# Carried rows of three state arrays moved channel-major straight between memory and their tiles

## The chip, the cores and the metric

The kernel runs on all 8 cores of one Trainium2 chip. Each core takes one prompt sequence of 2,048 tokens and 16 of the 128 sample sequences (64 tokens), and no core waits for another. The metric is the device time of the slowest of the 8 cores, in microseconds (us). Five runs here fell in a second, slower state, in which two or four cores of one die show a lower granted TensorE clock (0.812 to 0.975, against 0.986 or more on the other cores) and the time was 761.16 to 882.82 us; such runs are named and left out of every comparison.

The engines are PE (TensorE; PEld is its weight load, which overlaps the matmuls: busy 338.0 us beside PE's 700.8 us in a span of 744.3 us), DVE (VectorE), ACT (ScalarE), POOL (GpSimd) and SP (SyncE, which here mainly issues DMA). "L455" is line 455 of the kernel. Several such lines are helpers, so the same line stands for many places: in the kernel before, L455 is every matmul, L463 every transpose on PE, L480 the three-operand DVE operation, L484 an elementwise operation of two tensors, L491 a DVE operation with per-channel scalars.

## The reference, cut to what matters

One layer of a decoder with three kinds of carried state. Sample sequences bring the last 15 rows of a pooling mixer, the last 2 rows of a short convolution and the last 2 rows of the up-projected FFN, and each of these is handed back, renewed:

```python
def causal_dwconv(p, w):             # carried rows stand in front of the new ones
    T = p.shape[1] - (CONV_W - 1)    # CONV_W = 3
    out = p[:, 0:T] * w[0]
    for k in range(1, CONV_W):
        out = out + p[:, k:k + T] * w[k]
    return out

# in the layer
h = rmsnorm(x, g_pre_mix) * (1 + sc1) + sh1
proj = h @ w_in
pool_in = jnp.concatenate([pool_buf, v_pool], axis=1)           # 15 carried rows, 512 channels
conv_in = jnp.concatenate([conv_buf, gate_c * x_conv], axis=1)  # 2 carried rows, 512 channels
...                                                             # mixers, output projection
h2 = rmsnorm(x, g_pre_ffn) * (1 + sc2) + sh2
up = h2 @ ffn_w_up                                              # 2 x 2816 channels
ffn_in = jnp.concatenate([ffn_buf, up], axis=1)                 # 2 carried rows, 5632 channels
a, b = jnp.split(causal_dwconv(ffn_in, ffn_conv_w), 2, axis=-1)
f = (jax.nn.silu(a) * b) @ ffn_w_down
return x, pool_in[:, -15:], conv_in[:, -2:], ffn_in[:, -2:]
```

## The kernel before

In memory the states lie row by row: a row is one position, its channels side by side. On the chip channels lie on partitions. So the kernel before turns every state on PE, in float32, through a PSUM bank, with a copy by ACT; outgoing rows are also gathered by POOL and staged for the store. The FFN state and the outgoing rows of the pool and conv states look like this (cut):

```python
def ffn_states(m, g0, g1):                         # FFN state in, two calls
    K.dma("sp", ... BIG[m] <- stf_d ...)           # cut: four loads into a spare tile
    for c0 in range(g0, g1, 4):
        b = take()
        tr([PSF[:, b, ...] for c in range(c0, c1)], [BIG[m][:, ...] ...], IDF, ...)   # turns on PE
        ...
        act(USB[:, ..., 0:2], PSF[:, b, ...], AF.Copy, [r_bank[b]], [r_usb], ...)
        give(b)

def turn_out(rows, ins, reads, st):                # pool and conv rows out
    b = take()
    tr([PSF[0:rows, b, m * 128:(m + 1) * 128] for m in range(4)], ins, IDF, ...)
    act(STGO[st][0:rows, :], PSF[0:rows, b, :], AF.Copy, [r_bank[b]], [r_stgo[st]], 512)
    give(b)
```

The up projection: one half is 16 matmuls into a pair of PSUM banks. ACT copies it, scaled by the last tap of the convolution, and DVE adds the two other taps with one operation of 1,023 columns and one of 1,022. Only after the second may PE write the pair again. Per channel pair i there are two halves, called a and b below, and then a gate product on POOL:

```python
def up_half(gi, i, ab):
    b = take_pair()
    for c in range(2):
        op = mm(PSF[:, b + c, :], [(W[:, kc, w0:w0 + 128], AH[:, kc, c0:c0 + 512]) for kc in range(KC)], ...)
    ...
    act(Tt, ps, AF.Copy, ..., scale=f[2])
    act(hd, ps[:, 1022:1024], AF.Copy, ...)
    stt(Tt[:, 1:1024], ps[:, 0:1023], f[1], Tt[:, 1:1024], ALU.mult, ALU.add, ...)   # 1023 columns
    stt(Tt[:, 2:1024], ps[:, 0:1022], f[0], Tt[:, 2:1024], ALU.mult, ALU.add, ...)   # 1022 columns
    give(b, b + 1)                                                                   # the pair is free
    ...

ma = up_half(gi, i, 0)
act(BIG[ma], BIG[ma], AF.Silu, ...)
mb = up_half(gi, i, 1)
tt(GB[:, i, 0:1024], BIG[ma], BIG[mb], ALU.mult, ..., eng="pool")                    # the gate product
```

DVE still modulates later tokens of `ah`, the normed input of the up projection (`ah * g + s`, 512 columns of bfloat16 at a time).

What DVE does first is not written down by hand. Every operation is recorded with a modelled cost, and a list scheduler inside the kernel plays the program through and sets each engine's order from that.

```python
HOP = {"pe": 0.20, "act": 0.20, "dve": 0.15, "pool": 0.20, "sp": 0.10}

def order(self):
    ...
    for o in reversed(self.all):
        need[o] = o.idx if o.eng == "pe" else min([far] + [need[u] for u in users[o]])
        o.key = (need[o], o.idx)          # the PE operation that needs it first
    ...
    def done(o):
        o.end = t
        for u in users[o]:
            waiting[u] -= 1
            if not waiting[u]:
                push(t + (0.0 if o.eng == u.eng == "pe" else self.HOP[o.eng]), "ready", u)
    ...                                   # a free engine takes the ready operation with the lowest key
```

In this model an operation that depends on the one before it on DVE becomes ready 0.15 us late, and the engine, free by then, takes another that is ready.

## Time and profile before

| what | value |
|---|---|
| time, 4 runs | median 746.51 us (745.71 to 747.77) |
| spans of the 8 cores in the profiled run | 738.6 to 744.3 us |
| PE busy, slowest core | 700.8 of 744.3 us |
| float32 turns on PE | 51 |

The busy line and the chain of the page of the kernel before. The chain is followed back from the last instruction to whatever released each step; the shares are of the span:

```profile
span 744.3 us, 12312 instructions; the slowest of 8 cores (738.6 to 744.3 us)
PE 700.8 (94%) x4051; PEld 338.0 (45%) x4051; DVE 465.8 (63%) x624; ACT 334.7 (45%) x591; POOL 277.2 (37%) x297
...
PE 91%; DMA 3%; DVE 2%; issue 2%; ACT 1%; DVEq 0%; SPq 0%; ACTq 0%; POOLq 0%
```

PE is the bound. The table of stretches of the kernel before says where it is not: each row is a stretch, its length, then the busy time of PE, PEld, DVE, ACT and POOL with the count of instructions, the granted clock, the DMA share and GB/s:

```profile
80.00:120.00 40.00, 32.77 (x251) 17.32 (x250) 34.70 (x60) 26.61 (x52) 18.09 (x25) 1.00 0.98 169
120.00:260.00 140.00, 139.45 (x880) 69.56 (x878) 88.93 (x165) 75.06 (x151) 71.31 (x103) 0.99 0.80 201
260.00:690.00 430.00, 429.43 (x2326) 201.82 (x2325) 291.36 (x289) 184.82 (x289) 157.49 (x94) 1.00 0.43 94
690.00:744.00 54.00, 48.57 (x228) 22.55 (x226) 12.27 (x18) 10.25 (x24) 11.69 (x5) 0.97 0.34 110
```

From 120 to 690 us PE rests about 1.1 us. What a turn costs there is read from the timeline of PE in the kernel before (start, duration, engine, line, operation, count; matmuls overlap, here 0.27 us long and 0.11 us apart, so a slot is the distance between starts):

```profile
141.70 0.27 PE L463 MATMUL ps<-idf_51,v_119 128*15 128x128 f32 x1
141.81 0.27 PE L463 MATMUL ps<-idf_51,v_121 128*15 128x128 f32 x1
...
142.14 3.62 PE L455 MATMUL ps<-ah_81,ring_71 128*128 128x512 bf16 x16
```

A turn lasts 0.27 us but takes a slot of 0.11 us: starts at 141.70 and 141.81, and after four of them the next matmul at 142.14.

```profile
286.69 2.40 POOL L484 TENSOR_TENSOR g_137<-big_79,big_80 128x1024 bf16<-128x1024 f32 x1 [4.20 <-DVE big_80 L480]
```

The half in big_75 is finished (1,023 and 1,022 columns) before the half in big_76 begins. The modulation piece that starts before POOL's gate product takes 0.40 us (286.46); the one that starts within it takes 1.26 us (287.98) and ends 0.15 us after it (289.24 against 289.09).

### The profile page before, as it was taken

To read this page: it belongs to the slowest core of one execution; us is meant where nothing else is said; L and a number is where in the kernel's file an instruction comes from. 1 tells how busy PE (TensorE), PEld (TensorE's weight loads), DVE (VectorE), ACT (ScalarE), POOL (GpSimd) and SP (SyncE) were. 2 spreads that over 40 slices of the span, in tenths; PEclk is the share of its full clock that TensorE was granted. 3 is DMA by queue.
4 is the path that set the end of the run, shared out by engine and by line. 5 is a ranking of instruction groups with operands and counts; after the bars stand their busy time and mean duration, and the time that the engine had idled before them with its cause. 6 is when DMAs were issued, how large, how long until landed. Compare 5 with 4: busy or idle time off the path is not lost.

```text
span 744.3 us, 12312 instructions; the slowest of 8 cores (738.6 to 744.3 us)
## 1 busy us (share of the span) xinstructions
PE 700.8 (94%) x4051; PEld 338.0 (45%) x4051; DVE 465.8 (63%) x624; ACT 334.7 (45%) x591; POOL 277.2 (37%) x297
## 2 busy tenths in 40 slices
PE   1589888999999999999999999999999999999996
PEld 1244434544455544444444444445444444444443
DVE  2448686745468889987777511138777777767212
ACT  4526754533467784455454311134444444423211
POOL 2312333323488654434444232224434242342320
PEclk9979999999999999999999999999999999999999
DMA  8999999499687653355878943113344333032522
GB/s 206 187 215 222 184 172 158 91 181 210 185 284 254 215 155 73 58 94 92 165 136 156 216 144 114 56 57 58 57 81 91 58 58 57 1 114 86 168 86 70
DMA packets 28225, 97.94 MB, mean 132 GB/s; under 512 B 3283, under 2 KB 7723, under 8 KB 24562
## 3 DMA queue, kind: packets, MB, share of 16 engines
q0 software_dynamic: 10944, 47.85, 37.7%
q1 hardware_dynamic: 17218, 49.31, 20.3%
q8 instruction: 33, 0.54, 0.3%
q14 instruction: 30, 0.25, 0.1%
HBM read 126.15 MB, written 19.19 MB: 195 GB/s over the span
## 4 chain that ended last, share of the span: by engine, by line
PE 91%; DMA 3%; DVE 2%; issue 2%; ACT 1%; DVEq 0%; SPq 0%; ACTq 0%; POOLq 0%
PE ps L455 87%; PE ps L463 2%; PE ps L682 2%; DMA big_77<-x 2%; DMA wsc_2_85<-w_sc 2%; DVE ah_81 L489 0%; DVE by_82 L480 0%; ACT ah_81 L476 0%; DVE ah_81 L601 0%; DVE ta_107 L480 0%; DVE xn_99 L489 0%; SPq L495 0%; DVE big_79 L480 0%; ACT xn_100 L476 0%; DVE xn_101 L489 0%
## 5 line engine op out<-in xcount | busy, mean ns | idle before, releaser
L455 PE MATMUL ps<-wdn_136,g_137 128*128 128x512 bf16 (+1 forms) x748 | 162.8, 379 | 0.0
L455 PE MATMUL ps<-ah_81,ring_72 128*128 128x512 bf16 (+2 forms) x816 | 151.1, 341 | 2.2 <-DVE by_82 L480 2.2
L455 PE MATMUL ps<-ah_81,ring_71 128*128 128x512 bf16 (+2 forms) x784 | 149.1, 345 | 3.0 <-DVE ah_81 L484 1.1
L455 PE MATMUL ps<-ah_81,ring_70 128*128 128x512 bf16 (+2 forms) x752 | 139.6, 339 | 1.5 <-DVE big_79 L480 0.6
L455 PEld LDWEIGHTS ps<-wdn_136,g_137 128*128 128x128 bf16 (+1 forms) x748 | 73.3, 99 | 86.7 <-issue 0.8
L455 PEld LDWEIGHTS ps<-ah_81,ring_72 128*128 128x128 bf16 x816 | 69.1, 98 | 79.0 <-issue 5.1
L455 PEld LDWEIGHTS ps<-ah_81,ring_71 128*128 128x128 bf16 x784 | 67.5, 98 | 77.4 <-issue 4.3
L455 PEld LDWEIGHTS ps<-ah_81,ring_70 128*128 128x128 bf16 x752 | 63.5, 98 | 70.6 <-issue 2.6
L573 DVE RECIPROCAL stat_55<-stat_55 128x1 f32<-128x1 f32 (+1 forms) x67 | 10.4, 157 | 124.4 <-ACT stat_55 L476 124.1
L484 POOL TENSOR_TENSOR g_137<-big_75,big_76 128x1024 bf16<-128x1024 f32 x15 | 35.3, 2355 | 63.1 <-DVE big_76 L484 33.7
L484 POOL TENSOR_TENSOR g_137<-big_77,big_78 128x1024 bf16<-128x1024 f32 x15 | 35.3, 2354 | 58.5 <-DVE big_78 L484 33.1
L484 POOL TENSOR_TENSOR g_137<-big_79,big_80 128x1024 bf16<-128x1024 f32 x14 | 33.0, 2359 | 55.5 <-DVE big_80 L484 27.9
L476 ACT ACTIVATE big_80<-ps 128x1024 bf16<-128x1024 f32 (+2 forms) x16 | 15.5, 968 | 75.3 <-PE ps L455 65.0
L480 DVE SCALAR_TENSOR_TENSOR big_75<-ps,vecs_43,big_75 128x1023 f32<-128x1023 f32 (+1 forms) x30 | 38.4, 1280 | 12.6 <-ACT halo_57 L476 4.9
L480 DVE SCALAR_TENSOR_TENSOR big_77<-ps,vecs_43,big_77 128x1023 f32<-128x1023 f32 (+1 forms) x30 | 38.4, 1281 | 12.1 <-ACT halob_58 L476 6.7
L480 DVE SCALAR_TENSOR_TENSOR big_76<-ps,vecs_43,big_76 128x1023 f32<-128x1023 f32 (+1 forms) x30 | 38.4, 1279 | 9.6 <-ACT halob_58 L476 4.2
L480 DVE SCALAR_TENSOR_TENSOR big_79<-ps,vecs_43,big_79 128x1023 f32<-128x1023 f32 (+1 forms) x28 | 35.8, 1280 | 12.9 <-ACT halob_58 L476 7.6
L480 DVE SCALAR_TENSOR_TENSOR big_78<-ps,vecs_43,big_78 128x1023 f32<-128x1023 f32 (+1 forms) x30 | 38.4, 1279 | 7.7 <-ACT halob_58 L476 3.5
L480 DVE SCALAR_TENSOR_TENSOR big_80<-ps,vecs_43,big_80 128x1023 f32<-128x1023 f32 (+1 forms) x28 | 35.8, 1280 | 8.3 <-ACT halob_58 L476 3.9
L476 ACT ACTIVATE big_79<-ps 128x1024 bf16<-128x1024 f32 x14 | 14.3, 1022 | 52.5 <-PE ps L455 51.6
L484 POOL TENSOR_TENSOR big_76<-big_80,big_76 128x256 f32<-128x256 f32 (+1 forms) x16 | 21.0, 1310 | 33.9 <-DVE big_80 L480 32.8
L484 POOL TENSOR_TENSOR big_75<-big_79,big_75 128x256 f32<-128x256 f32 (+1 forms) x16 | 19.6, 1227 | 34.2 <-DVE big_79 L480 23.2
(353 smaller groups left out, 933.6 us busy)
## 6 DMA issues: line engine op xcount, KB each, us to landing
ring_70<-w_up POOLq DMA_DIRECT2D x8, 1024.0 KB, 8.1
ring_71<-w_up POOLq DMA_DIRECT2D x7, 1024.0 KB, 8.4
ring_72<-w_up POOLq DMA_DIRECT2D x7, 1024.0 KB, 8.1
wdn_136<-w_down POOLq DMA_DIRECT2D x11, 512.0 KB, 12.1
y<-big_75 SPq DMA_DIRECT2D x7, 512.0 KB, 2.7
y<-big_76 SPq DMA_DIRECT2D x7, 512.0 KB, 2.7
y<-big_77 SPq DMA_DIRECT2D x7, 512.0 KB, 2.8
big_76<-x SPq DMA_DIRECT2D x6, 512.0 KB, 6.6
```

What stands on the lines that cost most here:

```text
L455: inst = e.matmul(bank_ap, l, r, start=(first and i == 0), stop=(last and i == len(pairs) - 1))
L463: inst = e.transpose(o, i, ident)
L476: return K.op("act", lambda e: e.activation(out=out, in_=in_, func=func, **kw), reads=reads, writes=writes, cost=c_act(n, ptr))
L480: return K.op(eng, lambda e: e.scalar_tensor_tensor(out, in0, s, in1, op0, op1), reads=reads, writes=writes, cost=c_dve(n))
L484: return K.op(eng, lambda e: e.tensor_tensor(out, in0, in1, op), reads=reads, writes=writes, cost=c_dve(n) if eng == "dve" else c_pool(n))
L573: K.op("dve", lambda e: e.reciprocal(STAT[0:rows, k + 1, t:t + 1], STAT[0:rows, k + 1, t:t + 1]), reads=[r_stat[k + 1][t]], writes=[r_stat ...
L682: inst = e.matmul(PSF[:, start_b[g, c], :], WINP[:, kc, g * 128:(g + 1) * 128], AH[:, kc, c * 512:(c + 1) * 512], start=(kc == 0), stop=(k ...
```

## The change

Its intent: the host lays the three states out channel by channel, so that each tile, with carried and new rows together, moves in one load and one store. Turns, their PSUM banks, ACT and POOL copies, staging, 16 small stores and a memory-to-memory copy of pool rows go. The price is bytes, since whole tiles travel with unused columns: the FFN state moves 2.16 MB each way instead of 0.72. The steps of the input projection are written as a list as well; the program order of the steps is as before, but every engine's order is computed anew. The core of the diff (cut):

```diff
-    stf_d = din("st_ffn", [NS * 2, 2 * DFF])
+    stf_d = din("st_ffn", [128, NCH * NS * (2 + DS)])
     ...                                              (likewise the pool and conv states, and all outputs)
-    def state_turns():  ...                          (8 turns: pool state in)
-    def conv_state_turn():  ...                      (4 turns: conv state in)
-    def ffn_states(m, g0, g1):  ...                  (11 turns: FFN state in)
+    def conv_state_in():
+        load(QS.rearrange("p j s r -> p (j s r)"), stc_d, [r_qs], 196608, deps=[conv_op[0, 0]])
+    def pool_state_in():
+        load(VS.rearrange("p g s r -> p (g s r)"), stp_d, [r_vs], 622592, deps=[conv_op[0, 4]])
+    def ffn_state_in():
+        load(USB.rearrange("p i a s r -> p (i a s r)"), stf_d, [r_usb], 2162688, deps=[up_op[-1]])
     ...
     def conv_states():                               (8 turns; pool_states likewise, 8 turns)
-        turn_out(2, [QLAST[:, j, :] for j in range(4)], r_ql, 2)
-        store(ncp_d, STGO[2][0:2, :], [r_stgo[2]], s_stgo[2])
-        new = SS[1][:, 0:8 * NS].rearrange("p (g s r) -> p g s r", g=4, r=2)
-        K.op("pool", lambda e: e.tensor_copy(new, QS[:, :, :, 4:6]), reads=[r_qs], writes=[r_ss[1]], cost=0.4)
-        turn_out(2 * NS, [SS[1][:, g * 2 * NS:(g + 1) * 2 * NS] for g in range(4)], [r_ss[1]], 0)
-        store(ncs_d, STGO[0][0:2 * NS, :], [r_stgo[0]], s_stgo[0])
+        store(ncp_d, QLAST.rearrange("p j r -> p (j r)"), r_ql, nbytes=4096)
+        store(ncs_d, QS.rearrange("p j s r -> p (j s r)"), [r_qs], nbytes=196608)
     ...
-                if i == NTAIL + 1:
-                    ffn_states(7, 0, 8)              (inside the first half of the up projection)
-                if i == NTAIL + 4:
-                    ffn_states(7, 8, 11)
     ...
         if step == 2:                                (inside the first down projection)
+            ffn_state_in()
     ...
-    def state_outs(xs):  ...                         (12 turns: FFN rows out)
+    def state_outs():
+        store(nfp_d, HALOB.rearrange("p r c -> p (r c)"), [r_halob], nbytes=45056)
+        store(nfs_d, USB.rearrange("p i a s r -> p (i a s r)"), [r_usb], nbytes=2162688)
```

## The prediction

> **What bounds the kernel.** TensorE. The page gives PE 700.8 us of a 744.3 us span (94%); the chain of waits is 91% PE. By the table of stretches the 43.5 us in which PE does not work are: 21.7 before 26.5 us (first loads), 7.7 up to 80 us, 7.2 from 80 to 120 us (DVE busy 34.7 of 40 us), about 1.1 from 120 to 690 us, 5.7 at the end. So after 120 us TensorE time taken out should come off the end.
>
> **What goes.** All 51 float32 turns of state. The groups say about 272 ns for one, which would make 14 us. [...] back to back, turns start every 0.11 us (141.70, 141.81, 141.92, 142.03, then the next matmul at 142.14). So they cost 51 x 0.11 = 5.6 us: conv in 0.44 at 70 us, pool in 0.82 at 114 us, pool out 0.88 at 142 to 146 us, conv out 0.88 at 195 us, FFN in 1.2 at 343 and 364 us, FFN out 1.3 at 689 and 695 us. Off the path go about 6 us of ACT copies, 5.3 us of POOL copies, 16 small stores that hold SP's queue 7 us from 148 us, and a 352 KB memory-to-memory copy.
>
> **What comes.** Tiles travel whole with unused columns: FFN 2.16 MB each way instead of 0.72, pool 0.62 MB, conv 0.20 MB. Conv and pool in, together 0.26 MB more, fall where the DMA engines are full (share about 1.0 from 10 to 130 us). The hardware queue moved 49.3 MB for 20.3% of 16 engines' span, so I estimate 0.8 us of all engines for it. Neither is urgent: conv state was ready at 71 us and first used at 84.9 us; pool state was issued at 83.8 us, landed within 13 us, and was turned at 114 us. The FFN state lands during the down projection (DMA share about 0.4); FFN rows may leave from 660 us, 80 us before the last store. The rewritten list of projection steps reads as the same order as before: no gain.
>
> **On the path.** The 39 turns after 120 us give 4.3 us; the 0.5 us wait before the conv rows' turns may go too. Of the 1.26 us before 120 us I count half, as DVE holds that stretch and a 2.17 us wait on DVE follows the pool turns. Sum about 5 us, less 0.3 us for fuller DMA queues. The order of issues and of PSUM banks is computed anew from a model inside the kernel, so the first 120 us may shift 2 us either way.
>
> **Predicted: 742.0 us, 738.5 to 745.0 in 8 of 10. Faster by over 2%: 3%; within 2%: 95%; slower by over 2%: 2%.**
>
> **What would show it.** No float32 turns on PE; PE busy about 6 us lower (near 694); PE idle between 120 and 690 us still about 1 us; the span about 4 us shorter between 120 us and the end, whatever the first 120 us do. If those gained more, the order of loads was the reason.
>
> **What would make it wrong.** A store that must land before its tile's space is reused (pool rows before the output weights, conv rows before x tiles) holding the POOL queue, which also computes; larger loads delaying x tiles or modulation weights in the full stretch; the 2.16 MB FFN load holding residual tiles behind it; turns that hid in waits I do not see.

The 5.6 us are 51 times the 0.11 us between starts in the timeline.

## More of the kernel before

The next two views are the stretch to compare later. First PE in the kernel before, from the turns of a bfloat16 tile at 267 us to 336 us:

```profile
267.23 0.61 PE L463 MATMUL ps<-idb_52,xn_100 128*128 128x128 bf16 x8
...
280.64 7.08 PE L455 MATMUL ps<-ah_81,ring_71 128*128 128x512 bf16 x32
287.56 13.98 PE L455 MATMUL ps<-ah_81,ring_72 128*128 128x512 bf16 x64
301.37 13.98 PE L455 MATMUL ps<-ah_81,ring_70 128*128 128x512 bf16 x64
315.19 13.98 PE L455 MATMUL ps<-ah_81,ring_71 128*128 128x512 bf16 x64
329.00 7.29 PE L455 MATMUL ps<-ah_81,ring_72 128*128 128x512 bf16 x33
```

Each row of 64 matmuls is four halves, and nothing stands in brackets after it: no wait that this view shows. Then the timeline of DVE in the same kernel, and below it one row of POOL's:

```profile
286.46 0.40 DVE L491 TENSOR_SCALAR ah_81<-ah_81,g2t_49,s2t_50 128x512 bf16<-128x512 bf16 x1
286.79 1.27 DVE L480 SCALAR_TENSOR_TENSOR big_75<-ps,vecs_43,big_75 128x1023 f32<-128x1023 f32 x1
287.98 1.26 DVE L491 TENSOR_SCALAR ah_81<-ah_81,g2t_49,s2t_50 128x512 bf16<-128x512 bf16 x1
289.16 1.27 DVE L480 SCALAR_TENSOR_TENSOR big_75<-ps,vecs_43,big_75 128x1022 f32<-128x1022 f32 x1
290.35 1.27 DVE L480 SCALAR_TENSOR_TENSOR big_76<-ps,vecs_43,big_76 128x1023 f32<-128x1023 f32 x1
```

## The result, and the profile after

The kernel after took 744.42 us (median of 4 runs, 743.72 to 745.17) against 746.51 us (4 runs, 745.71 to 747.77), a ratio of 0.9971 with a 95% interval of 0.9951 to 0.999. A ratio here is always the mean time of one kernel's fast runs over that of the other's of the same rounds, so it is not quite the ratio of the medians. The gain is about 2 us, less than half of what was predicted, and the time lies inside the range given.

The page of the kernel after, same lines as before:

```profile
span 742.2 us, 12030 instructions; the slowest of 8 cores (740.4 to 742.2 us)
PE 691.0 (93%) x3925; PEld 332.7 (45%) x4000; DVE 469.2 (63%) x624; ACT 328.1 (44%) x576; POOL 271.4 (37%) x293
...
PE 84%; DVE 5%; issue 5%; DMA 3%; ACT 1%; POOL 1%; DVEq 0%; SPq 0%; ACTq 0%; POOLq 0%
```

The weight loads fell from 4051 to 4000: exactly the 51 turns. The matmuls do not fit to that (3925), so 75 matmul records are missing from this trace and its PE busy time, 691.0, must not be compared with 700.8. The chain of waits is the better witness: PE's share of it fell from 91% to 84%, DVE's rose from 2% to 5% (that of "issue", which names no cause, rose as much).

The table of stretches after (same columns; the PE column is short of records here too):

```profile
80.00:120.00 40.00, 33.04 (x232) 16.70 (x237) 33.39 (x59) 25.43 (x51) 15.28 (x24) 0.96 1.04 186
120.00:260.00 140.00, 137.23 (x856) 68.36 (x870) 94.19 (x173) 75.64 (x152) 71.66 (x103) 1.00 0.81 202
260.00:690.00 430.00, 425.14 (x2264) 199.76 (x2307) 291.69 (x283) 182.02 (x282) 152.41 (x92) 1.00 0.49 104
690.00:744.00 54.00, 45.78 (x209) 20.97 (x211) 11.37 (x17) 7.34 (x18) 11.19 (x5) 0.98 0.26 88
```

Since weight loads are complete, they make a ruler without this flaw. The table below cuts each core's span at the first and last weight loads of the output projection and of the two down projections. All its rows but the start and the tail agree across the 8 cores of a run within 0.15 us, so they can be compared to a tenth; the tail differs by up to 0.5 us between cores after the change. Values are medians of the 8 cores of the profiled run.

| stretch, us | turns in it (before) | before | after | difference | predicted |
|---|---|---|---|---|---|
| start, to the output projection | 20 | 188.3 (185.2 to 190.9) | 188.6 (187.7 to 189.1) | see below | about -1.5 |
| output projection | 8 | 65.51 | 64.50 | -1.01 | -0.9 |
| first half of the up projection | 11 | 156.43 | 158.06 | **+1.63** | -1.2 |
| first down projection | 0 | 75.76 | 75.76 | 0.00 | 0 |
| second half of the up projection | 0 | 162.05 | 162.05 | 0.00 | 0 |
| second down projection | 12 | 87.30 | 85.99 | -1.31 | -1.3 |
| tail | 0 | 6.33 | 6.41 | +0.08 | 0 |

Here is the miss, in one row. The first half of the up projection (from the last weight load of the output projection to the first of the down projection) lost 11 turns and became longer. This is PE in that stretch after the change; a bracket is the time PE rested before a row, and what released it:

```profile
264.44 0.61 PE L476 MATMUL ps<-idb_52,xn_100 128*128 128x128 bf16 x8
...
284.77 3.62 PE L468 MATMUL ps<-ah_81,ring_72 128*128 128x512 bf16 x16
289.47 10.52 PE L468 MATMUL ps<-ah_81,ring_72 128*128 128x512 bf16 x47 [1.09 <-DVE big_75 L493]
299.83 3.62 PE L468 MATMUL ps<-ah_81,ring_70 128*128 128x512 bf16 x16
304.17 10.52 PE L468 MATMUL ps<-ah_81,ring_70 128*128 128x512 bf16 x47 [0.72 <-DVE big_79 L493]
314.52 3.62 PE L468 MATMUL ps<-ah_81,ring_71 128*128 128x512 bf16 x15
318.68 10.52 PE L468 MATMUL ps<-ah_81,ring_71 128*128 128x512 bf16 x47 [0.54 <-DVE big_77 L493]
329.04 7.29 PE L468 MATMUL ps<-ah_81,ring_72 128*128 128x512 bf16 x33
```

Compare the two ends with the view before. At the bfloat16 turns of xn_100 this core is 2.79 us ahead (264.44 against 267.23). At the last row it is level (329.04 against 329.00). In between three groups of 64 matmuls have each broken into 16 and 48 (a record or two are missing in each) with a wait for DVE. The brackets understate the waits, because ends of matmuls are modelled: between weight loads the gaps are 1.65, 1.28 and 1.10 us, where the usual distance is 0.22.

And this is the timeline of DVE in the kernel after, with one row of POOL's below it:

```profile
282.99 2.76 DVE L504 TENSOR_SCALAR ah_81<-ah_81,g2t_49,s2t_50 128x512 bf16<-128x512 bf16 x2
285.67 1.27 DVE L493 SCALAR_TENSOR_TENSOR big_75<-ps,vecs_43,big_75 128x1023 f32<-128x1023 f32 x1
286.87 1.27 DVE L493 SCALAR_TENSOR_TENSOR big_76<-ps,vecs_43,big_76 128x1023 f32<-128x1023 f32 x1
288.06 1.26 DVE L493 SCALAR_TENSOR_TENSOR big_75<-ps,vecs_43,big_75 128x1022 f32<-128x1022 f32 x1
289.25 1.26 DVE L493 SCALAR_TENSOR_TENSOR big_76<-ps,vecs_43,big_76 128x1022 f32<-128x1022 f32 x1
```

```profile
283.21 2.39 POOL L497 TENSOR_TENSOR g_135<-big_79,big_80 128x1024 bf16<-128x1024 f32 x1 [4.19 <-DVE big_80 L493]
```

Two things differ from before. The pieces are *crossed*: the 1,023 columns of big_76 now stand between the two pieces of big_75, so the PSUM pair of big_75 comes free one piece (1.2 us) later. And two modulation pieces in a row took 2.76 us: the first its usual time, while the second, alone in the trace from 283.31 to 285.75, began just after POOL's gate product and ended just after it (283.21 to 285.60). Measured from the start of the ring_72 matmuls, the pair came free after 2.87 us before (290.43 - 287.56) and after 4.55 us now (289.32 - 284.77), which is 1.68 us later. The 16 matmuls of the other half, which PE does meanwhile, take 3.45 us (a quarter of the 13.81 us between rows of 64): before, the pair was free in time, and now PE stood still until 289.47.

The crossing occurs at three pairs of halves, counted from 0 in program order: 6 and 7, 10 and 11, 14 and 15. The kernel before has none there. The full order of DVE in the trace adds a hint that no run tested: before, one modulation piece stands between the two pieces of nearly every half in this part; after, at the three places, two modulation pieces stand together in front of the halves, and none is left to stand between.

**Theory.** The turns did give back their slots, but the newly computed order crosses half-convolutions on DVE at three places and puts modulation pieces against POOL's gate product, and PE waits for PSUM there.

**Rivals.** (R1) The stretch is bound by DVE (busy 60.6 of the 65 us from 264 to 329 us before), so turns hid in DVE's time and taking them out frees nothing. (R2) The larger transfers hold others up. (R3) The order is accidental and a nudge of PE's modelled time restores it.

### The profile page after: what moved, and what is told of

Read it like the earlier page. It is cut to its first block, busy times and chain, and to the rows that moved or that the text cites. A ratio compares the mean times of both kernels' runs of the same rounds, so it can differ in the third digit from the quotient of the medians.

```text
span 742.2 us, 12030 instructions; the slowest of 8 cores (740.4 to 742.2 us)
## 1 busy us (share of the span) xinstructions
PE 691.0 (93%) x3925; PEld 332.7 (45%) x4000; DVE 469.2 (63%) x624; ACT 328.1 (44%) x576; POOL 271.4 (37%) x293
## 4 chain that ended last, share of the span: by engine, by line
PE 84%; DVE 5%; issue 5%; DMA 3%; ACT 1%; POOL 1%; DVEq 0%; SPq 0%; ACTq 0%; POOLq 0%
PE ps L468 81%; PE ps L695 2%; DMA wsc_2_85<-w_sc 2%; PE ps L476 2%; DMA big_77<-x 1%; DVE big_75 L493 1%; DVE big_79 L493 1%; POOL big_77 L497 0%; DVE ta_107 L493 0%; DVE big_80 L493 0%; DVE ah_81 L502 0%; DVE ah_81 L504 0%; ACT ah_81 L489 0%; DVE by_82 L493 0%; DVE xn_99 L502 0%
## 5 line engine op out<-in xcount | busy, mean ns | idle before, releaser
L468 PE MATMUL ps<-wdn_134,g_135 128*128 128x512 bf16 (+1 forms) x733 | 161.4, 379 | 0.9 <-issue 0.2
L468 PE MATMUL ps<-ah_81,ring_71 128*128 128x512 bf16 (+2 forms) x766 | 148.5, 346 | 5.6 <-DVE ah_81 L502 2.2
L468 PE MATMUL ps<-ah_81,ring_72 128*128 128x512 bf16 (+2 forms) x798 | 148.4, 338 | 2.2 <-DVE big_75 L493 1.1
L468 PE MATMUL ps<-ah_81,ring_70 128*128 128x512 bf16 (+2 forms) x739 | 138.0, 339 | 3.2 <-DVE ah_81 L502 0.9
L489 ACT ACTIVATE big_79<-ps 128x1024 bf16<-128x1024 f32 x14 | 14.3, 1023 | 55.8 <-PE ps L468 54.8
L497 POOL TENSOR_TENSOR big_75<-big_79,big_75 128x256 f32<-128x256 f32 (+1 forms) x16 | 20.0, 1250 | 49.6 <-DVE big_79 L493 30.9
L468 PE MATMUL ps<-wo_138,by_82 128*128 128x512 bf16 (+1 forms) x134 | 31.9, 379 | 0.1
```

Source lines behind the costliest of these rows:

```text
L468: inst = e.matmul(bank_ap, l, r, start=(first and i == 0), stop=(last and i == len(pairs) - 1))
L489: return K.op("act", lambda e: e.activation(out=out, in_=in_, func=func, **kw), reads=reads, writes=writes, cost=c_act(n, ptr))
L497: return K.op(eng, lambda e: e.tensor_tensor(out, in0, in1, op), reads=reads, writes=writes, cost=c_dve(n) if eng == "dve" else c_pool(n))
```

## The experiments

All kernels gave correct results. Two sessions were run, each on one chip and each with runs of the kernel before. In the first session (e1 to e4) the kernel before had a median of 746.28 us (5 fast runs; 2 slow ones of 815.51 and 882.82 are left out); in the second (e5 to e7 and after_again) 746.42 us (11 runs, 745.94 to 748.2). The first measurement above is apart from both. "The stretch" is the first half of the up projection, measured as in the table: 156.43 us before, 158.06 us after.

### e1_uncrossed: the kernel after, with the three crossings undone

```diff
+        dve = self.ops["dve"]
+        for k in (6, 10, 14):
+            b, a = self.halves[k][1], self.halves[k + 1][0]   # 1022 of one half, 1023 of the next
+            if dve.index(b) > dve.index(a):
+                dve.remove(b)
+                dve.insert(dve.index(a), b)
```

> The changed kernel with one edit: after the order of issue is computed, the three crossed pairs of half-convolutions on DVE in the first half of the up projection (a-first, b-first, a-second, b-second) are put straight (a-first, a-second, b-first, b-second). Nothing else moves. The stretch from the last weight load of the output projection to the first of the down projection was 156.4 us before and 158.1 us after, on all 8 cores. Theory A (the crossings hold PSUM pairs and so TensorE): the waits of 1.65, 1.28 and 1.10 us start-to-start shrink to under 0.5 us and the stretch is 155 to 155.6 us (before less the 1.2 us of turns); the whole kernel about 2.5 us faster than after (ratio to before about 0.993 to 0.995). Theory B (DVE is full in this stretch and TensorE waits for it in any order): the stretch stays within 0.7 us of 158.1.

Measured: the stretch 156.22 us, 1.84 us shorter; the other stretches as in the kernel after within 0.1 us. This lies between the two forecasts, nearer to theory A but outside its 155 to 155.6 us. Time 743.85 us, the median of the 3 fast runs (742.92 to 744.28, one slow run of 761.16 left out), ratio to the kernel before 0.996 (0.9936 to 0.9984). PE in this run (tile names have no numbers in the traces of experiments, and the lines lie a little lower with each edit):

```profile
280.51 10.53 PE L475 MATMUL ps<-ah,ring 128*128 128x512 bf16 x48
291.25 13.97 PE L475 MATMUL ps<-ah,ring 128*128 128x512 bf16 x64 [0.20 <-DVE big L500]
305.63 30.64 PE L475 MATMUL ps<-ah,ring 128*128 128x512 bf16 x141 [0.41 <-DVE big L500]
```

What follows: moving three DVE instructions ahead of a neighbour gives back 1.84 of the 2.83 us that the stretch lacks (158.06 less the 155.23 that it has in e5_ffn_in below, with its turns gone and nothing else). Crossing is a cause, but not all of it: gaps of 0.76 and 0.98 us stay at the first two places, and one of 0.45 us comes later, at 332.8 us.

### e2_crossed: the kernel before, with the same three pairs crossed

```diff
+        for k in (6, 10, 14):
+            b, a = self.halves[k][1], self.halves[k + 1][0]
+            dve.remove(b)
+            dve.insert(dve.index(a) + 1, b)
```

> The kernel before with one edit: after the order is computed, the same three pairs of half-convolutions on DVE (7th and 8th, 11th and 12th, 15th and 16th half) are crossed as they are after the change. All turns stay. Theory A: the stretch from output to down projection grows from 156.4 us by 1 to 3 us, with waits of TensorE on DVE at those three places, and nothing else changes. Theory B: it stays at 156.4 within 0.3 us.

Measured: the stretch 158.94 us, 2.51 us longer; all turns stay in. Time 751.2 us, the median of the 3 fast runs (748.18 to 751.55, one slow run of 778.97 left out), ratio 1.0052 (1.0018 to 1.0086). PE in this run:

```profile
282.94 10.53 PE L462 MATMUL ps<-ah,ring 128*128 128x512 bf16 x48
294.20 13.97 PE L462 MATMUL ps<-ah,ring 128*128 128x512 bf16 x64 [0.72 <-DVE big L487]
308.82 13.97 PE L462 MATMUL ps<-ah,ring 128*128 128x512 bf16 x64 [0.65 <-DVE big L487]
```

What follows: the crossing alone makes the waits, with not a byte and not a turn changed. So the waits need no larger transfer (R2). Nor do they need longer modulation pieces: the 19 pieces in the stretch sum to 12.68 us here and to 15.30 us in the kernel before. The stretch accounts for 2.5 us; the time rose by more, and the part beyond 2.5 us lies in the start (up to 193.2 us in this profile) and in the tail (6.78 against 6.33 us), which the edit does not touch.

### e3_phantom: the kernel after, with modelled PE time put back where the turns of the conv rows stood

```diff
     def conv_states():
+        for _ in range(2):
+            K.op("pe", None, deps=[<the last PE operation>], cost=1.2)    # no instruction, only modelled time
         store(ncp_d, ...)
```

> The changed kernel, with two entries added for TensorE in the kernel's own model at the place of the removed conv-row turns: they take 1.2 us each in the model and issue no instruction. If the removed turns changed the order through the model (a faster TensorE in the model, so a DVE further behind in it), the computed order moves back towards that of before: as built it has one crossing in place of three. Theory A: the stretch is then about 156 us, 2 us shorter than after, with one wait left. Theory B: it stays near 158.1 us.

Measured: the stretch 157.61 us; one crossing instead of three; time 743.23 us (one run). Against it, PE now waits 2.00 us for a normed tile 18 us into the stretch, where no other kernel waits. The expectation of about 156 us was wrong, though its count of crossings was right. So R3 fails in this form: the nudge did move the order, but to another uneven one, 2.4 us worse than 155.2. It does show that modelled costs alone, with no change of work, change the order and its waits: two crossings went and a wait of 2.00 us came, 0.45 us net.

### e4_tail: the kernel before, with only the FFN rows out moved directly

```diff
-        K.op("pool", lambda e, ab=ab: e.tensor_copy(STO[...], USB[:, :, ab, :, 4:6]) ...)
-        tr(...); act(...); dma(...)                      (12 turns, their copies and stores)
+        store(nfp_d, HALOB.rearrange("p r c -> p (r c)"), [r_halob], nbytes=45056)
+        store(nfs_d, USB.rearrange("p i a s r -> p (i a s r)"), [r_usb], nbytes=2162688)
```

> The kernel before with one part of the change alone: FFN rows out go channel-major straight from their tiles (2.16 MB store, no 12 turns, no copies). As built, TensorE's order differs by those turns alone. If a turn costs its 0.11 us slot where TensorE is full, the last down-projection stretch falls from 87.30 to 86.0 us, and everything before it stays (output to down projection 156.4 us). If the larger store delayed residual tiles or output, the time after the last matmul (6.3 us) would grow by over 1 us.

Measured: the second down projection 85.99 us against 87.30, the tail 6.60 against 6.33, everything else as before (the stretch 156.43). Time 745.24 us (one run). What follows: 12 turns are worth 1.31 us, 0.109 us each, and the larger store costs the tail 0.3 us at most. (Even that is not shown to be the store: the tail of e2_crossed, whose stores are those of the kernel before, is 6.78 us.)

### e5_ffn_in: the kernel before, with only the FFN state in moved directly

```diff
-                if i == NTAIL + 1:
-                    ffn_states(7, 0, 8)
-                if i == NTAIL + 4:
-                    ffn_states(7, 8, 11)
     ...
+            load(USB.rearrange("p i a s r -> p (i a s r)"), stf_d, [r_usb], 2162688, deps=[up_op[-1]])
```

> The kernel before with one part of the change alone: FFN state in, loaded whole (2.16 MB) channel-major into its tile, without the 11 turns. As built no pair of half-convolutions is crossed in the first half of the up projection. If the time of the turns is there to be had whenever the DVE order stays good, the stretch from output to down projection falls from 156.43 us to 155.2 us (less 11 x 0.11 us) and no other stretch moves by over 0.2 us. If the larger load were the cost, the down-projection stretch after it (75.76 us) or the second up stretch (162.06 us) would grow.

Measured: the stretch 155.23 us, 1.20 us shorter; the first down projection, during which the 2.16 MB land, 75.76 us as before; time 745.78 us (one run). In the built order no pair is crossed. What follows: the 11 turns are worth 1.20 us in the stretch, exactly as predicted, when the order stays. R1 fails: DVE's load did not hide them. R2 fails for the largest load. The kernel as a whole shows little of it, 0.64 us against the median of the kernel before, which one run cannot settle.

### e6_conv_ffn: the kernel before, with the conv rows out and the FFN state in moved directly

```diff
+        store(ncp_d, QLAST.rearrange("p j r -> p (j r)"), r_ql, nbytes=4096)        (in place of 8 turns)
+        store(ncs_d, QS.rearrange("p j s r -> p (j s r)"), [r_qs], nbytes=196608)
     ...                                                                            (and e5_ffn_in's edit)
```

> The kernel before with two parts of the change: conv rows out and FFN state in. Each alone gives, as built, no crossed pair; both together give the three crossings of the changed kernel (7th, 11th and 15th half). The order theory expects the output-projection stretch 1 us shorter (about 64.5 us against 65.5) and the stretch from output to down projection near 158 us, as after the change, though 11 turns are gone from it. A theory of turns and transfers alone expects 155.2 us.

Measured: the stretch 158.37 us with gaps of 1.78, 1.28 and 1.28 us at the same three places; the output projection 64.44 us against 65.51, as in the kernel after; time 748.13 us (one run). The conv rows go out before the stretch begins and have no instruction in it. What follows: two parts, each without a crossing when done alone, bring the crossing of 6, 10 and 14 when done together. The loss belongs to the combination, through the computed order. It also comes without the rewritten list of projection steps, which this kernel does not have.

Built orders without a run say the same and no more: the kernel before has no crossing among these halves; with conv rows out alone, none; with the FFN state in alone, none; with both, 6, 10 and 14; with pool and conv rows out, 0, 4 and 8. Setting the modelled cost of all turns of the kernel before to zero crosses none, so the cause is not that cost by itself.

### e7_spaced: e1_uncrossed, with the modulation pieces spread away from POOL's gate product

```diff
+        first = dve.index(self.halves[5][0])
+        late = [o for o in dve[first:] if o in self.mods]      # pieces not yet issued at half 5
+        for i, o in enumerate(late):
+            dve.remove(o)
+            k = 7 + i // 2 * 2
+            dve.insert(dve.index(self.halves[k][i % 2]), o)    # one before each piece of halves 7, 9, 11, ...
```

> The changed kernel with the three pairs uncrossed, and the modulation pieces of the later tokens (wanted only in the second half of the up projection) moved on DVE to just before the two half-convolutions of each second half, where POOL's gate product of the pair before should have ended. In the profile after the change such a piece lasts 0.40 us alone and up to 2.44 us when it starts with POOL's product, ending with it. Theory: this blocking is what the uncrossed kernel still lost (156.22 us against 155.2 expected). Then the pieces all last about 0.4 us, the waits of 0.5 to 0.8 us at those places go, and the stretch is 154.5 to 155.3 us; the kernel runs 3 us faster than the changed one and about 5 us faster than before (ratio to before about 0.993). Rival (what is left is DVE's own work): the stretch stays within 0.4 us of 156.2.

Measured: the stretch 155.23 us. Time 741.57 us, the median of the 5 fast runs (740.38 to 743.25, one slow run of 849.15 left out), ratio to the kernel before 0.9934 (0.9919 to 0.9949). PE in this run, then the row of 264 to 329 us from the table of stretches, and two modulation pieces from the timeline of DVE:

```profile
278.74 58.45 PE L482 MATMUL ps<-ah,ring 128*128 128x512 bf16 x270
```

```profile
264.00:329.00 65.00, 65.00 (x320) 29.94 (x319) 57.21 (x61) 38.17 (x57) 26.86 (x17) 1.00 0.45 90
```

```profile
286.39 0.40 DVE L518 TENSOR_SCALAR ah<-ah,g2t,s2t 128x512 bf16<-128x512 bf16 x1
288.40 0.40 DVE L518 TENSOR_SCALAR ah<-ah,g2t,s2t 128x512 bf16<-128x512 bf16 x1
```

One row of 270 matmuls without a wait. In the same window DVE was busy 60.61 us in the kernel before, 60.39 after and 61.23 in e1_uncrossed, and 57.21 here, with about the same instructions (59 to 62). The last 12 modulation pieces sum to 6.56 us against 13.13 us in e1_uncrossed: 9 of them take 0.40 us, 3 still take 0.98 us, and the longest in e1_uncrossed took 2.44. What follows: the rest of the loss after uncrossing came from where the modulation pieces stood, and with both mended the stretch has its whole gain of 1.2 us. That it was their overlap with POOL's product (in the kernel after 0.40 us outside one, 2.44 us inside) is the likely reason, and the durations speak for it; but the edit also takes apart pieces that stood two in a row, and no run separates the two. This version beats both kernels.

### after_again: the kernel after, unchanged, as a control for the second session

> The changed kernel itself, as a control beside the one above and for a closer figure of the change: ratio to before about 0.997, the stretch from output to down projection 158.1 us.

Measured: 746.16 us median of 6 runs (744.49 to 746.84), ratio 0.9992 (0.998 to 1.0003), which does not exclude that the change gains nothing; 0.997 was expected. The stretches are those of the first profile within 0.15 us (64.43, 158.21, 75.76, 162.12, 85.99, 6.35). What follows: by medians the first measurement puts the whole change at 2.1 us and the second session at 0.3; e7_spaced, beside it on the same chip, is at 4.85 us. Against this kernel it is 4.6 us faster, of which 2.98 us lie in the stretch (158.21 - 155.23); the rest is in no other stretch after the start, so it must lie in the start. The difference between the two measurements of the change is not in any stretch after the start either.

## Why the prediction was wrong

The prediction said 742.0 us, a gain of about 4.5 us; the first measurement gave 2.1 and the second session 0.3 (medians). Point by point:

- **PE is the bound, and a turn costs its slot, not its duration: right.** The trace has means of 270 to 273 ns for float32 turns of the form 128x128 (265 and 266 for 120x120, 227 for 32x32); what the time consists of no run here shows. The slot is shorter: e4_tail gives 1.31 us for 12 turns, e5_ffn_in 1.20 us for 11, which is 0.109 us each against the predicted 0.11.
- **FFN rows out, 1.3 us: right** (1.31 in the kernel after and in e4_tail). **Conv rows out, 0.88 us and perhaps the wait before them: right** (1.01).
- **Bigger tiles cost almost nothing: right.** The first down projection carries the 2.16 MB load at 75.76 us in both kernels. The 0.3 us set aside for it were not needed; the tail rose 0.08 us, less than it varies between runs.
- **The start, about 1.5 us (half of the 1.26 us before 120 us, and the pool rows out at 0.88): about right in size, but buried.** See below; no run shows by which route the start gained, since its turns and its order changed together.
- **FFN state in, 1.2 us: wrong, and here the whole miss of the first measurement lies.** "The 39 turns after 120 us give 4.3 us" failed in this term: the stretch became 1.63 us longer instead of 1.2 us shorter, 2.83 us off. "PE idle between 120 and 690 us still about 1 us" fails with it: the three gaps alone are 1.65, 1.28 and 1.10 us. Summed over all stretches after the start, the change gave 0.61 us (-1.01 + 1.63 - 1.31 + 0.08) where 3.4 had been counted.

The step that failed is the assumption that the rest of the order stays as it was after 120 us. The prediction did write that the order of issues is computed anew, but let that move only the first 120 us; after them it took PE, at nearly 100%, as the one bound ("after 120 us TensorE time taken out should come off the end"). In effect a full PE was taken for slack on the others. It was not: DVE was busy 60.6 of 65 us there, and it fed PE just in time (the pair of the half in big_75 was free after 2.87 us, and PE was done with the other half after 3.45). In this stretch an order on DVE that was one piece off at three places became waits on PE. Uncrossing alone gives back 1.84 us, uncrossing and spacing 2.83 us, crossing the kernel before costs 2.51 us: that part is shown, not argued.

The second part, about 1 us, goes with the place of the modulation pieces. A modulation piece takes 0.40 us outside POOL's gate product (281.48 to 281.88 in the kernel after) and 2.44 us when it begins together with one (283.31 to 285.75, POOL 283.21 to 285.60), while a half-convolution keeps its 1.27 us inside such a product (286.79 to 288.06 in the kernel before, POOL 286.69 to 289.09). By what mechanism the piece is held no run shows. From 266 to 330 us the 15 modulation pieces of the slowest core sum to 11.97 us before and to 15.50 us after. Before, pieces of up to 1.55 us made no wait on PE.

**Why the start hides the rest.** The start differs between cores of one run (185.2 to 190.9 us in the profiled run before, 187.7 to 189.1 after): some cores have a stretch of half clock from about 34 to 48 us. In the traces of the two kernels a drop to half clock in the start lasts 3.41, 6.83 or 13.65 us; what sets it off no run shows. In the profiled runs of kernels that keep the order of the start of the kernel before, the 12 cores with 13.7 us and no further drop up to 100 us take 179.5 us from their first weight load to the output projection, and the 15 cores with none take 175.9 us: 3.6 us less, 0.5% of 745 us and more than the 2.1 us of the first measurement. In those with the order of the kernel after, 26 cores with 13.7 us take 177.9 us: like with like, the start gained about 1.65 us, near the predicted 1.5, though it may owe this to its new order as well as to the turns. But the time is that of the slowest of 8 cores, and in each of the 10 profiled runs at least one core has the drop. In the first profile after 7 of 8 cores had it, in the one before 3.

**What stays open.** Which modelled term tips the order over: only that the combination of conv rows out and FFN state in does it. Whether the half clock is the cause of the longer start or follows from a late PE: it goes with it, and no run changed it on purpose. Whether the change makes the drop more frequent: by the mean clock of the fast runs (below 0.991) 43 of 88 cores show it before and 22 of 48 after in the second session, but 9 of 40 before in the first session and 19 of 32 after in the first measurement; in the profiled runs 15 of 40 cores with the start's order of before have the long drop, and 26 of 40 with that of after. So it may, and the runs do not settle it. And why the second session shows a smaller gain than the first measurement: the stretches after the start agree, so it must be the start, but no experiment separates it further. Last, how much of the second part is the overlap with POOL and how much is pieces that stand two in a row.

## What to carry to other kernels

When a kernel computes its own issue order from a model, a change of one part is a change of every order: before you predict, and again before you measure, compare the order of the engine that runs nearly full with that of the kernel before, place by place, in stretches that the change does not touch. Here PE, busy all 65 us of a stretch, beside DVE, busy 60.6 us of it (93%), was two bounds, not one bound and slack: taking 11 turns from PE made the stretch 1.20 us shorter where DVE's order held (e5_ffn_in) and 1.94 us longer where three pairs were crossed (e6_conv_ffn). And if a clean removal does not pay, look first for pairs of pieces that have changed places, and for short DVE operations that now start inside a long POOL operation (here modulation pieces, 0.40 us outside POOL's gate product and up to 2.44 us inside it); moving a few DVE instructions by some places gave 2.8 us in one stretch here, more than the whole change.
